# A hybrid decoder trunk: the even layer's mixer over all tokens at once, heads between later column blocks, three classical tiles instead of six

## The chip, the cores and the metric

The kernel runs on one core of one Trainium2 chip. The metric is the device time of one execution in microseconds. Three runs of the kernel before are given, and one execution was recorded by the hardware profiler.

## What is computed

The input x has 1024 tokens of 1024 channels, all in float32. Two layers follow each other, then a last RMS norm. Layer 0 has a mixer with one input projection of 2560 columns: differential attention (four heads, each with two softmax maps over 64 channels, and values of 128 channels) and four groups of spatial gating (a 128x128 lower-triangular product over each chunk of 128 tokens). Layer 1 has a convolution mixer. After each mixer comes a gated feed-forward block. The parts that the change touches, cut from the reference:

```python
def even_mixer(h, ...):
    proj = h @ w_in
    q, k, v = ...                       # 512, 512 and 512 columns
    uz = jax.nn.gelu(proj[..., o2:])    # 1024 columns
    u, z = jnp.split(uz, 2, axis=-1)
    q, k = apply_rope(q, cos, sin), apply_rope(k, cos, sin)
    o = diff_attention(q, k, v, lam)    # softmax(q1 k1) - lam * softmax(q2 k2), causal, times v
    o = rms_norm(o, subln_g) * (1.0 - lambda_init)
    g = spatial_gating(u, z, sg_ln_g, sg_ln_b, sg_w, sg_b)
    return jnp.concatenate([o, g], axis=-1) @ w_out

def conv_ffn(h, w_up, dw_w, dw_b, w_down):
    hh = causal_dwconv(h @ w_up, dw_w, dw_b)
    a, gate = jnp.split(hh, 2, axis=-1)
    return (a * jax.nn.silu(gate)) @ w_down

for l in range(2):
    x = x + mixer(rms_norm(x, norm_mix_g[l]), ...)
    x = x + conv_ffn(rms_norm(x, norm_ffn_g[l]), ...)
return rms_norm(x, final_norm_g)
```

## The kernel before

Tokens stand in eight tiles of 128 (`t`), four to a chunk `c` of 512. Every float32 matmul is made of three: each operand is split into a rounded high part (a cast on ACT, L144) and the rest (a subtraction on POOL or DVE, L148), and the products high-high, high-low and low-high are added in PSUM (`PASSES`).

*Column blocks.* `col_steps` streams a block of 512 weight columns: four loads of 1024 values a partition (`raw`), split into eight tiles `hl`, of which there are eight (`WHL`). Then each token tile is one step: 24 matmuls of 128x512 into one `bank` (L269), and a function `fin` that takes the bank away. A `fin` may return a second part (transposes and stores for queries and keys, L378 and L382; the gating product, L508). It is held in the list `delayed` and is done after three more steps, or when `flush` empties the list. The second parts write to one buffer `sec` and from there to DRAM. Each block of the mixer (values, two of queries and keys, two of gates) is streamed once for chunk 0 and once for chunk 1.

*Heads.* `att_steps(c, h)` has four units, one for each token tile of the chunk. A unit makes the scores of both maps on PE (L432, L435, mask L434), takes the maximum on DVE (L438, L440), the exp on ACT (L446), combines the maps on DVE (L455), transposes on PE (L462), copies on ACT (L463), and multiplies with the values on PE (L466). The first unit of a head calls `flush` and loads queries, keys and values from DRAM.

*Order of the work.* `interleave(main, shadow, start, end)` calls the steps of `main` and, spread over the given share of them, those of `shadow`. A scheduler then sets the order in which each engine's instructions stand. In layer 0: values for chunk 0, queries and keys, gates, the norm of chunk 1; then the heads of chunk 0 beside four blocks; then the output projection of chunk 0, the norm of its rows, the gates of chunk 1 and the first four feed-forward tiles, beside the heads of chunk 1.

*Feed-forward.* `head_steps` makes a tile of 128 hidden channels in the classical way: gate and value, 24 matmuls each for each chunk (L306), so 96. `pair_steps` makes a tile with seven products of 12 matmuls (L677), so 84. It needs sums and differences of normed rows; `combos` loads the rows `xd`, scales them again with the kept factors `rn`, and forms them. The first `PRE0` tiles of layer 0 are classical.

```python
    interleave(qk_steps(0, 1) + v_steps(1) + qk_steps(1, 0) + qk_steps(1, 1),
               [f for h in range(4) for f in att_steps(0, h)] + og_steps(0), 0.0, 0.85)
    open_psum(2)
    interleave(out_steps(ab_w_out[0], ogT, 0, x_from(x_in)) +
               norm_steps(0, xtile, norm_ffn_g[0], hF0, hb=sbank, keep=rn[0], spill=xd[0]) +
               gate_steps(1, 0) + gate_steps(1, 1) + head_steps(0, 0, hF0, order(0)[:PRE0 - PRE0_LATE]),
               [f for h in range(4) for f in att_steps(1, h)] + [flush] + og_steps(1), 0.0, 0.9)
```

`open_psum(wide)` divides the eight banks of PSUM anew: with 1 there are four single banks for column steps, one double and two small ones; with 2 there are two single banks and two double ones (the scores stand in a double one).

Of the kernel before, what the change touches and what calls it, by code (L numbers as in the profile page):

```python
# [10 lines left out]
F32 = mybir.dt.float32  # L11
# [9 lines left out]
P = 128  # L21
# [25 lines left out]
PRE0, PRE0_LATE = 6, 2  # L47
# [12 lines left out]
def trunk_kernel(ctx: ExitStack, tc: tile.TileContext, x, norm_mix_g, norm_ffn_g, ab_w_in, ab_w_out,  # L60
# [68 lines left out]
    def rows_to_cols(dst, loads):  # L129

        n = sum(c for _, c in loads)
        st = wk.tile([P, P], F32, tag="rtc", name="rtc", bufs=2)
        r = 0
        for ap, c in loads:
            nc.sync.dma_start(out=st[r:r + c, :], in_=ap)
            r += c
        ps = sbank()
        nc.tensor.transpose(ps[:, :n], st[:n, :], ident[:n, :n])
        nc.vector.tensor_copy(out=dst, in_=ps[:, :n])
# [51 lines left out]
    def rms_tile(xt, gain, junk, out=None, keep=None):  # L191
        ss = small.tile([P, 1], F32, tag="ss", name="ss")
        nc.scalar.activation(out=junk, in_=xt.rearrange("p (j c) -> p j c", c=P), func=AF.Square, accum_out=ss)
        r = rstd_of(ss, 1.0 / D, 1, "n", keep)
# [32 lines left out]
    def norm_steps(c, src, gain_ap, dst, in_place=False, hb=None, keep=None, spill=None):  # L227


        def f(t):  # L230
# [5 lines left out]
            if spill is not None:  # L236
                nc.sync.dma_start(out=spill[t * P:(t + 1) * P, :], in_=xt)
            xn = rms_tile(xt, dst["gain"], junk, xt if in_place else None, None if keep is None else keep[:, t:t + 1])
# [9 lines left out]
    def col_steps(load, hT, c, fin, early=False):  # L248
# [15 lines left out]
        def mm(t, late):  # L264
            ps = bank()
            n = 0
            for d in range(DT):
                for sa, sw in PASSES:
                    nc.tensor.matmul(ps, lhsT=hT[c][:, sa, d, tok(t)], rhs=units[d][:, sw, :],  # L269
# [6 lines left out]
        steps = [lambda t=t: f(t) for t in range(c * TPC, (c + 1) * TPC)]  # L276
# [46 lines left out]
    rn = [const.tile([P, NT], F32, name=f"rn{l}") for l in range(2)]  # L323
# [18 lines left out]
    def v_steps(c, early=False):  # L342
        return col_steps(plain_cols(w_in, 1024), hT0, c, v_fin, early)

    ns, vs = norm_steps(0, x_load, norm_mix_g[0], hT0, True, sbank), v_steps(0, True)
    ns[0]()
    vs[0]()
    for i in range(1, TPC):
        ns[i]()
        vs[i]()  # L350
    vs[TPC]()
# [128 lines left out]
    def gate_fin(j):  # L480
        st = {}

        def f(ps, t):
            if t % TPC == 0:
# [34 lines left out]
    def qk_steps(c, hp):  # L519
        return col_steps(two_cols(w_in, hp * 256, 512 + hp * 256), hT0, c, qk_fin(hp))  # L520

    def gate_steps(c, j):
        return col_steps(two_cols(w_in, 1536 + j * 256, 2048 + j * 256), hT0, c, gate_fin(j))
# [12 lines left out]
    def out_steps(w, actT, c, prepare, after=None):  # L536
# [9 lines left out]
        return [f for half in range(2) for f in col_steps(plain_cols(w, half * 512), actT, c, fin(half))]  # L546
# [66 lines left out]
    def combos(l, hT, up_pool):  # L613
# [4 lines left out]
        def f(k):  # L618
            if k == 0:
                T["gain"] = load_gain(norm_ffn_g[l])  # L620
# [258 lines left out]
    mf = wk.tile([P, P], F32, tag="rtc", name="rtc", bufs=2)  # L879
# [26 lines left out]
    for g in range(4):  # L906
        st = wk.tile([P, P], F32, tag="rtc", name="rtc", bufs=2)
# [163 lines left out]
    for c in range(NCH):  # L1071
# [12 lines left out]
    interleave(norm_steps(0, xtile, norm_ffn_g[1], hF1, keep=rn[1], spill=xd[1]) +  # L1084
# [4 lines left out]
               norm_steps(1, xtile, norm_ffn_g[1], hF1, keep=rn[1], spill=xd[1]), 0.0, 0.3)  # L1089
# [81 lines left out]
```

## Time and profile before

| | us |
|---|---|
| median of three runs (2303.5 to 2309.1) | 2305.05 |
| the profiled execution's own time | 2305.63 |
| its span | 2303.9 |
| PE busy | 2147.5 (93%) |
| DVE busy | 1601.8 (70%) |
| ACT busy | 1120.9 (49%) |
| POOL busy | 1002.2 (43%) |

A matmul's busy time counts its whole passage, and matmuls follow each other faster than that, so a stretch in which PE is always busy can still hold slow matmuls: the granted clock of the stretch tells. Times inside the execution are counted from the span's start.

### The profile page before, as it was taken

The page shows a single profiled execution, that of the slowest core. Times are in us where ns is not written, and L with a number is a line of the kernel's source. Part 1 is how long each engine was busy: PE and PEld are TensorE (multiplying, and loading weights), DVE is VectorE, ACT ScalarE, POOL GpSimd, SP SyncE. Part 2 cuts the span into 40 slices and gives each one's busy share as a digit, 9 for nine tenths or more (in the row PEclk, how much of TensorE's full clock was granted, in tenths as well). Part 3 has the DMA queues.
Part 4 walks back from the last instruction along what each step waited for, and adds up shares of the span by engine and source line. Part 5 has one row for each costly group of instructions (what it writes and reads, how often), then busy time and mean ns, then how long its engine had stood idle before and what let it go on. Part 6 is the DMA issues. An engine that isn't in the chain of part 4 may idle for free.

```text
span 2303.9 us, 28559 instructions
## 1 busy us (share of the span) xinstructions
PE 2147.5 (93%) x9882; PEld 1760.4 (76%) x9882; DVE 1601.8 (70%) x2787; ACT 1120.9 (49%) x1971; POOL 1002.2 (43%) x824
## 2 busy tenths in 40 slices
PE   8889879989999999999999969979989899999987
PEld 6677768778788888888887758858768788878876
DVE  6675747864875555555699968996576576766676
ACT  4344535642445444443556566555533444544354
POOL 3312311222635444445579836974555455530011
PEclk9999979999999999999999979979989999999999
DMA  7736545435432222275634422523535233339423
GB/s 240 217 101 202 172 151 185 156 97 193 142 100 80 92 84 82 85 247 191 192 113 125 152 78 83 155 69 115 183 118 161 78 111 96 116 118 328 128 89 112
DMA packets 299953, 318.80 MB, mean 138 GB/s; under 512 B 12445, under 2 KB 221601, under 8 KB 299297
## 3 DMA queue, kind: packets, MB, share of 16 engines
q1 hardware_dynamic: 293920, 302.30, 41.0%
q0 software_dynamic: 5888, 14.68, 2.1%
q8 instruction: 78, 1.28, 0.2%
q14 instruction: 67, 0.54, 0.1%
HBM read 253.76 MB, written 63.18 MB: 138 GB/s over the span
## 4 chain that ended last, share of the span: by engine, by line
PE 70%; DVE 18%; issue 4%; DMA 3%; ACT 3%; POOL 3%; SPq 0%; ACTq 0%; DVEq 0%; POOLq 0%
PE bank L677 25%; PE bank L306 14%; PE bank L269 11%; PE bank L821 7%; PE bank L858 6%; DVE sbank L1006 5%; DVE hl L148 2%; PE sbank L821 2%; DVE y L182 1%; POOL ap L1003 1%; PE sbank L466 1%; POOL hl L148 1%; DVE xn L197 1%; PE sbank L213 1%; ACT hl L144 1%
## 5 line engine op out<-in xcount | busy, mean ns | idle before, releaser
L148 POOL TENSOR_TENSOR hl<-raw,hl 128x512 fp32r<-128x512 f32 x456 | 632.0, 1404 | 506.4 <-ACT hl L144 479.5
L306 PE MATMUL bank<-big,hl 128*128 128x512 f32 x2112 | 498.8, 395 | 9.5 <-DVE big L225 3.4
L144 ACT CAST hl<-raw 128x512 fp32r<-128x512 f32 x616 | 358.2, 618 | 233.9 <-PE bank L858 68.9
L306 PEld LDWEIGHTS bank<-big,hl 128*128 128x128 f32 x2112 | 396.9, 190 | 95.6 <-DVE big L225 5.0
L269 PE MATMUL bank<-hl,big 128*128 128x512 f32 x1728 | 427.4, 402 | 20.5 <-POOL hl L148 9.2
L269 PEld LDWEIGHTS bank<-hl,big 128*128 128x128 f32 x1728 | 325.9, 192 | 91.2 <-POOL hl L148 9.8
L677 PE MATMUL bank<-big,hl 128*128 128x512 f32 x1440 | 342.9, 390 | 0.1
L677 PEld LDWEIGHTS bank<-big,hl 128*128 128x128 f32 x1440 | 270.0, 188 | 58.2 <-ACT hl L144 0.5
L677 PE MATMUL bank<-t,hl 128*128 128x512 f32 x1080 | 264.2, 394 | 6.0 <-ACT hl L144 6.0
L1006 DVE SCALAR_TENSOR_TENSOR sbank<-yb,cw,sbank 128x512 f32<-128x512 f32 x352 | 248.1, 748 | 6.0 <-ACT sbank L995 3.2
L685 DVE SCALAR_TENSOR_TENSOR bank<-row,dw,bank 128x1024 f32<-128x1024 f32 x120 | 154.5, 1287 | 140.6 <-ACT bank L683 138.1
L858 PE MATMUL bank<-hl 128*128 128x512 f32 x1056 | 247.1, 392 | 2.5 <-DVE hl L148 2.2
L677 PEld LDWEIGHTS bank<-t,hl 128*128 128x128 f32 x1080 | 203.6, 189 | 51.2 <-ACT hl L144 6.3
L148 DVE TENSOR_TENSOR hl<-raw,hl 128x512 fp32r<-128x512 f32 x160 | 169.6, 1080 | 93.1 <-ACT hl L144 92.8
L858 PEld LDWEIGHTS bank<-hl 128*128 128x128 f32 x1056 | 196.4, 188 | 48.8 <-DVE hl L148 8.4
L821 PE MATMUL bank<-hl 128*128 128x512 f32 x726 | 176.8, 398 | 10.4 <-DVE s L731 4.4
L821 PEld LDWEIGHTS bank<-hl 128*128 128x128 f32 x726 | 139.4, 193 | 42.3 <-issue 5.8
L1003 POOL TENSOR_TENSOR ap<-ap,pr 128x512 f32<-128x512 f32 x112 | 153.8, 1373 | 34.5 <-ACT ap L998 20.7
L144 ACT CAST hl<-s 128x512 fp32r<-128x512 f32 x101 | 62.8, 621 | 137.6 <-DVE s L700 75.3
L579 DVE SCALAR_TENSOR_TENSOR s<-bank,dw,s 128x510 f32<-128x510 f32 x112 | 83.5, 745 | 52.9 <-ACT s L576 51.4
L1002 ACT ACTIVATE pr<-yb,cw 128x512 f32<-128x512 f32 x112 | 80.8, 723 | 70.2 <-POOL ap L1003 70.0
L1112 POOL TENSOR_TENSOR xr<-xr,gain 128x512 f32<-128x512 f32 x10 | 14.5, 1479 | 202.3 <-ACT xn L1104 176.8
(206 smaller groups left out, 2565.8 us busy)
## 6 DMA issues: line engine op xcount, KB each, us to landing
raw<-in_ffn_w_up SPq DMA_DIRECT2D x116, 512.0 KB, 4.1
raw<-in_ffn_w_down SPq DMA_DIRECT2D x44, 512.0 KB, 3.8
raw<-phd SPq DMA_DIRECT2D x44, 512.0 KB, 4.8
ph<-phs SPq DMA_DIRECT2D x33, 512.0 KB, 3.5
raw<-in_ab_w_in SPq DMA_DIRECT2D x64, 256.0 KB, 3.5
raw<-in_conv_w_in SPq DMA_DIRECT2D x32, 512.0 KB, 4.1
qd<-s SPq DMA_DIRECT2D x32, 256.0 KB, 2.9
qk<-qd POOLq DMA_DIRECT2D x8, 1024.0 KB, 7.0
```

Of the source, the lines that this page charges most:

```text
L144: nc.scalar.copy(out=hl_hi, in_=raw)
L148: eng.tensor_sub(out=hl_lo, in0=raw, in1=hl_hi.bitcast(F32))
L269: nc.tensor.matmul(ps, lhsT=hT[c][:, sa, d, tok(t)], rhs=units[d][:, sw, :], start=(n == 0), stop=(n == 3 * DT - 1))
L306: nc.tensor.matmul(ps, lhsT=hv[d // 4][:, sw, d % 4, :], rhs=hT[:, sa, d, :], start=(n == 0), stop=(n == 3 * DT - 1))
L579: nc.vector.scalar_tensor_tensor(out=y[:, sh:], in0=ps[:, :CH - sh], scalar=dw[:, k, ct:ct + 1], in1=y[:, sh:], op0=ALU.mult, op1=ALU.add)
L677: nc.tensor.matmul(ps, lhsT=hv[:, sw, d, :], rhs=B[n](sa, d), start=(start and i == 0), stop=(i == 11), skip_group_check=True)
L685: nc.vector.scalar_tensor_tensor(out=y, in0=r[:, k:k + S], scalar=dw[:, k, ct:ct + 1], in1=y, op0=ALU.mult, op1=ALU.add)
L821: nc.tensor.matmul(ps[k], lhsT=a[:, sa, k * P:(k + 1) * P], rhs=w[:, sw, :], start=(n in (5, 2, 1) and js[0] == 0 and i == 0), stop=(end a ...
L858: nc.tensor.matmul(ps, lhsT=phs[i][:, sa, k * P:(k + 1) * P], rhs=wds[i][:, sw, :], start=(dp == 0 and n == 0), stop=(dp == DP - 1 and n = ...
L1002: nc.scalar.activation(out=pr, in_=ys[ct][:, k:k + CH], func=AF.Copy, scale=cw[:, ct, k:k + 1])
L1003: nc.gpsimd.tensor_add(out=st["ap"], in0=st["ap"], in1=pr)
L1006: nc.vector.scalar_tensor_tensor(out=st["acc"], in0=ys[ct][:, k:k + CH], scalar=cw[:, ct, k:k + 1], in1=st["acc"], op0=ALU.mult, op1=ALU.add)
```

## The change

The mixer's blocks are streamed once, each for all eight token tiles: values beside the norm of all eight, then queries and keys of the first two heads, and from then on the heads of both chunks, head by head, beside the second block of queries and keys and the two blocks of gates. PSUM is divided anew before the heads. The output projections and the norms follow after the heads. Three tiles of layer 0's feed-forward are classical instead of six. The norm writes its result to a DRAM tensor `xnd`, and `combos` loads that instead of scaling again; its four subtractions are all on DVE, where two were on POOL. There are four `rtc` buffers instead of two.

```diff
-PRE0, PRE0_LATE = 6, 2
+PRE0 = 3
...
-        st = wk.tile([P, P], F32, tag="rtc", name="rtc", bufs=2)
+        st = wk.tile([P, P], F32, tag="rtc", name="rtc", bufs=4)
...
             if spill is not None:
-                nc.sync.dma_start(out=spill[t * P:(t + 1) * P, :], in_=xt)
-            xn = rms_tile(xt, dst["gain"], junk, xt if in_place else None, None if keep is None else keep[:, t:t + 1])
+                nc.sync.dma_start(out=spill[0][t * P:(t + 1) * P, :], in_=xt)
+            xn = rms_tile(xt, dst["gain"], junk, xt if in_place else None)
+            if spill is not None:
+                nc.sync.dma_start(out=spill[1][t * P:(t + 1) * P, :], in_=xn)
             transpose_split(xn, dst[c], t, hb)
...
-    def col_steps(load, hT, c, fin, early=False):
+    def col_steps(load, hT, ts, fin, early=False):
...
-                    nc.tensor.matmul(ps, lhsT=hT[c][:, sa, d, tok(t)], rhs=units[d][:, sw, :],
+                    nc.tensor.matmul(ps, lhsT=hT[t // TPC][:, sa, d, tok(t)], rhs=units[d][:, sw, :],
...
-        steps = [lambda t=t: f(t) for t in range(c * TPC, (c + 1) * TPC)]
+        steps = [lambda t=t: f(t) for t in ts]
...
-    ns, vs = norm_steps(0, x_load, norm_mix_g[0], hT0, True, sbank), v_steps(0, True)
+    ns = [f for c in range(NCH) for f in norm_steps(c, x_load, norm_mix_g[0], hT0, True, sbank)]
+    vs = col_steps(plain_cols(w_in, 1024), hT0, range(NT), v_fin, True)
...
-                nc.sync.dma_start(out=xt, in_=xd[l][t * P:(t + 1) * P, :])
-                nc.vector.scalar_tensor_tensor(out=xt, in0=xt, scalar=rn[l][:, t:t + 1], in1=T["gain"],
-                                               op0=ALU.mult, op1=ALU.mult)
+                nc.sync.dma_start(out=xt, in_=xnd[t * P:(t + 1) * P, :])
...
-            nc.gpsimd.tensor_sub(out=xb[:, :512], in0=xb[:, 512:], in1=xb[:, :512])
+            nc.vector.tensor_sub(out=xb[:, :512], in0=xb[:, 512:], in1=xb[:, :512])
...
-            nc.gpsimd.tensor_sub(out=xa[:, 512:], in0=xa[:, 512:], in1=xb[:, 512:])
+            nc.vector.tensor_sub(out=xa[:, 512:], in0=xa[:, 512:], in1=xb[:, 512:])
...
-    run(qk_steps(0, 0))
-    run(gate_steps(0, 0))
-    interleave([f for pair in zip(gate_steps(0, 1), norm_steps(1, x_load, norm_mix_g[0], hT0, True, sbank)) for f in pair],
-               const_steps())
-    interleave(qk_steps(0, 1) + v_steps(1) + qk_steps(1, 0) + qk_steps(1, 1),
-               [f for h in range(4) for f in att_steps(0, h)] + og_steps(0), 0.0, 0.85)
+    interleave(qk_steps(0), const_steps())
     hF0 = {}
-    flush()
     open_psum(2)
-    interleave(out_steps(ab_w_out[0], ogT, 0, x_from(x_in)) +
-               norm_steps(0, xtile, norm_ffn_g[0], hF0, hb=sbank, keep=rn[0], spill=xd[0]) +
-               gate_steps(1, 0) + gate_steps(1, 1) + head_steps(0, 0, hF0, order(0)[:PRE0 - PRE0_LATE]),
-               [f for h in range(4) for f in att_steps(1, h)] + [flush] + og_steps(1), 0.0, 0.9)
-    run(out_steps(ab_w_out[0], ogT, 1, x_from(x_in)))
-    interleave(head_steps(0, 0, hF0, order(0)[PRE0 - PRE0_LATE:PRE0]),
-               norm_steps(1, xtile, norm_ffn_g[0], hF0, keep=rn[0], spill=xd[0]), 0.0, 0.3)
+    att = [att_steps(c, h) for h in range(4) for c in range(NCH)]
+    g1 = gate_steps(1)
+    interleave(qk_steps(1) + gate_steps(0) + g1[:TPC], [f for a in att[:7] for f in a], 0.08, 1.0)
+    interleave(g1[TPC:] + [flush], att[7] + og_steps(0), 0.0, 1.0)
+    interleave(out_steps(ab_w_out[0], ogT, 0, x_from(x_in)), og_steps(1), 0.0, 0.8)
+    interleave(out_steps(ab_w_out[0], ogT, 1, x_from(x_in)),
+               norm_steps(0, xtile, norm_ffn_g[0], hF0, hb=sbank, spill=(xd[0], xnd)), 0.0, 0.8)
     M.close()
     open_psum(1)
+    interleave(head_steps(0, 0, hF0, order(0)[:PRE0]),
+               norm_steps(1, xtile, norm_ffn_g[0], hF0, spill=(xd[0], xnd)), 0.0, 0.4)
```

How instructions stand after the scheduler, at two places. On PE, inside a head of the second chunk, before the change (L269 are column matmuls of the output projection, L432 and L435 scores, L462 transposes, L466 products with the values):

```order
L269 MATMUL bank<-hl,big 128x512 x6
L466 MATMUL sbank<-vh,aT 128x128 x4
L462 MATMUL sbank<-ident,e 128x128 x4
L269 MATMUL bank<-hl,big 128x512 x13
L432 MATMUL bank_3721<-qk 128x448
L435 MATMUL bank_3721<-qk 128x448
L432 MATMUL bank_3721<-qk 128x448
L434 LDWEIGHTS identb
```

After the change, on PE, the same part of such a head (the second head's last unit):

```order
L462 MATMUL sbank<-ident,e 128x128 x4
L466 MATMUL sbank<-vh,aT 128x128
L432 MATMUL bank_2763<-qk 128x512
L435 MATMUL bank_2763<-qk 128x512
L432 MATMUL bank_2763<-qk 128x512
L434 LDWEIGHTS identb
L434 MATMUL bank_2763<-maskb,identb 128x128
L435 MATMUL bank_2763<-qk 128x512
L462 MATMUL sbank<-ident,e 128x128 x2
L432 MATMUL bank_2772<-qk 128x512
```

Column matmuls stood between a head's transposes and its next scores, and now they don't. They stand in bursts at other places, as here, in the third head (L271 is L269 before, L508 the gating product):

```order
L508 MATMUL bank<-held,sgwT 128x128 x2
L271 MATMUL bank<-hl,big 128x512 x47
L462 MATMUL sbank<-ident,e 128x128 x3
L271 MATMUL bank<-hl,big 128x512
L508 MATMUL bank<-held,sgwT 128x128 x2
L466 MATMUL sbank<-vh,aT 128x128 x3
L462 MATMUL sbank<-ident,e 128x128 x4
```

So a whole head of the second chunk may pass with hardly a column matmul, and then two steps of a block follow at once. On ACT, in the fourth head of the first chunk after the change (L492 is the gates' gelu, L446 the heads' exp; each ACT_TABLE_LOAD changes the function table):

```order
L492 ACT_TABLE_LOAD
L492 ACTIVATE held<-bank 128x512
L463 COPY aT<-sbank 128x512
L463 COPY aT<-sbank 128x384
L446 ACT_TABLE_LOAD
L446 ACTIVATE e,sm<-bank_3677,nm 128x256 x2
L492 ACT_TABLE_LOAD
L492 ACTIVATE held<-bank 128x512
```

Gates and heads alternate on ACT: up to the first pair tile there are 27 table loads, where there were 16.

## Rows read from the trace of the kernel before

**Rows 1.** The page: span, and shares of the chain of waits by engine.

```profile
span 2303.9 us, 28559 instructions
...
PE 70%; DVE 18%; issue 4%; DMA 3%; ACT 3%; POOL 3%; SPq 0%; ACTq 0%; DVEq 0%; POOLq 0%
```

**Rows 2.** Busy time by stretch (us); columns are named in its first line.

```profile
core 0: us, PE busy (x) PEld busy (x) DVE busy (x) ACT busy (x) POOL busy (x), PEclk, DMA share, GB/s
0.00:136.60 136.60, 117.38 (x556) 95.43 (x557) 93.84 (x299) 57.83 (x106) 42.45 (x45) 0.98 0.66 209
136.60:516.00 379.40, 333.90 (x1814) 278.67 (x1813) 248.35 (x613) 188.37 (x426) 89.97 (x80) 0.93 0.50 155
136.60:328.00 191.40, 157.67 (x831) 129.96 (x830) 108.08 (x238) 79.35 (x214) 46.30 (x46) 0.88 0.56 173
328.00:486.00 158.00, 146.23 (x824) 123.04 (x823) 127.68 (x352) 92.48 (x180) 34.66 (x27) 0.98 0.46 145
375.00:475.00 100.00, 88.23 (x498) 74.00 (x496) 89.57 (x282) 66.95 (x124) 25.11 (x20) 0.97 0.52 161
516.00:682.70 166.70, 161.93 (x768) 133.35 (x768) 113.25 (x181) 65.70 (x107) 69.82 (x50) 1.00 0.47 149
750.00:1050.00 300.00, 300.00 (x1316) 246.78 (x1315) 171.75 (x200) 143.38 (x220) 126.02 (x118) 1.00 0.36 121
```

**Rows 3.** Waits of PE, 136.6 to 516 us: us in total, times, longest.

```profile
PE sbank L466 <- DVE big L217: 7.8, 1, 7.8
...
PE bank L378 <- ACT s L379: 7.3, 2, 6.1
...
PE bank L432 <- ACT e L446: 6.7, 5, 2.9
...
PE bank L382 <- DVE s L364: 5.1, 1, 5.1
```

**Rows 4.** Timeline of PE: start, us, instructions, idle before and its releaser.

```profile
11.03 8.25 PE L269 MATMUL bank<-hl,big 128*128 128x512 f32 x24 [0.62 <-ACT big L216]
...
110.77 1.65 PE L269 MATMUL bank<-hl,big 128*128 128x512 f32 x3 [5.51 <-POOL hl L148]
...
136.60 0.31 PE L432 MATMUL bank<-qk 128*128 128x128 f32 x1
...
515.74 15.24 PE L306 MATMUL bank<-big,hl 128*128 128x512 f32 x66
...
530.82 1.91 PE L221 MATMUL bank<-ident,ot 128*128 128x128 f32 x16
...
682.71 1.64 PE L677 MATMUL bank<-big,hl 128*128 128x512 f32 x6
```

**Rows 5.** Timeline of DVE: the heads' first maximum and the last two.

```profile
141.21 0.42 DVE L440 TENSOR_REDUCE nm<-bank 128x2 f32<-128x256 f32 x1
...
484.93 2.35 DVE L438 TENSOR_REDUCE nm<-bank 128x1 f32<-128x1024 f32 x2
```

**Rows 6.** Groups of DVE and POOL to 690 us: busy us, mean ns, idle before.

```profile
L438 DVE TENSOR_REDUCE nm<-bank 128x1 f32<-128x1024 f32 x8 | 9.7, 1218 | 2.8 <-PE bank L435 2.8
...
L384 DVE COPY sec<-bank 128x512 f32<-128x512 f32 x16 | 11.0, 686 | 15.4 <-DMA kd<-sec 9.3 <-PE bank L382 6.1
...
L629 DVE SCALAR_TENSOR_TENSOR s<-s,rn,gain 128x1024 f32<-128x1024 f32 x4 | 7.2, 1798 | 0.2 <-DMA s<-xd 0.2
...
L629 DVE SCALAR_TENSOR_TENSOR xa<-xa,rn,gain 128x1024 f32<-128x1024 f32 x4 | 6.1, 1536 | 0.3 <-DMA gain<-in_norm_ffn_g 0.3
...
L635 DVE TENSOR_TENSOR s<-s,xa 128x512 f32<-128x512 f32 x4 | 4.9, 1221 | 0.3 <-POOL s L634 0.3
...
L636 POOL TENSOR_TENSOR xa<-xa,s 128x512 f32<-128x512 f32 x4 | 6.1, 1530 | 0.6 <-DVE s L635 0.6
```

**Rows 7.** Timeline of ACT at a table load.

```profile
391.23 1.28 ACT L492 ACT_TABLE_LOAD   x1
392.53 0.60 ACT L492 ACTIVATE held<-bank 128x512 f32<-128x512 f32 x1
```

More of the change, by code (lines that the diff above doesn't have):

```diff
@@ L189, in rstd_of, with rms_tile @@
         return out
-    def rms_tile(xt, gain, junk, out=None, keep=None):
+    def rms_tile(xt, gain, junk, out=None):
         ss = small.tile([P, 1], F32, tag="ss", name="ss")
         nc.scalar.activation(out=junk, in_=xt.rearrange("p (j c) -> p j c", c=P), func=AF.Square, accum_out=ss)
-        r = rstd_of(ss, 1.0 / D, 1, "n", keep)
+        r = rstd_of(ss, 1.0 / D, 1, "n")
         if out is None:
@@ L225, in transpose_split, with norm_steps @@
         nc.vector.tensor_sub(out=dst[:, 1, :, tok(t)], in0=psv, in1=hi.bitcast(F32))
-    def norm_steps(c, src, gain_ap, dst, in_place=False, hb=None, keep=None, spill=None):
+    def norm_steps(c, src, gain_ap, dst, in_place=False, hb=None, spill=None):
         def f(t):
@@ L322, in trunk_kernel @@
     phs = dram.tile([P, 7, HH, CH], F32, name="phs")
-    rn = [const.tile([P, NT], F32, name=f"rn{l}") for l in range(2)]
+    xnd = dram.tile([S, D], F32, name="xnd")
     M = ExitStack()
@@ L340, in v_fin @@
         nc.sync.dma_start(out=vd[t * P:(t + 1) * P, :], in_=vt)
-    def v_steps(c, early=False):
-        return col_steps(plain_cols(w_in, 1024), hT0, c, v_fin, early)
-    ns, vs = norm_steps(0, x_load, norm_mix_g[0], hT0, True, sbank), v_steps(0, True)
+    ns = [f for c in range(NCH) for f in norm_steps(c, x_load, norm_mix_g[0], hT0, True, sbank)]
+    vs = col_steps(plain_cols(w_in, 1024), hT0, range(NT), v_fin, True)
     ns[0]()
     vs[0]()
-    for i in range(1, TPC):
+    for i in range(1, NT):
         ns[i]()
         vs[i]()
-    vs[TPC]()
+    vs[NT]()
     def qk_fin(hp):
@@ L483, in f @@
         def f(ps, t):
-            if t % TPC == 0:
+            if t == 0:
                 lngb = mp.tile([P, 2, 256], F32, tag="lngb", name="lngb", bufs=1)
@@ L517, in gate_fin, with qk_steps, gate_steps @@
         return f
[L519 to L523, printed above, removed]
+    def qk_steps(hp):
+        return col_steps(two_cols(w_in, hp * 256, 512 + hp * 256), hT0, range(NT), qk_fin(hp))
+    def gate_steps(j):
+        return col_steps(two_cols(w_in, 1536 + j * 256, 2048 + j * 256), hT0, range(NT), gate_fin(j))
     ogT = {}
@@ L545, in fin @@
             return f
-        return [f for half in range(2) for f in col_steps(plain_cols(w, half * 512), actT, c, fin(half))]
+        return [f for half in range(2) for f in col_steps(plain_cols(w, half * 512), actT, range(c * TPC, (c + 1) * TPC), fin(half))]
     dws, halos = [], []
@@ L619, in f @@
             if k == 0:
-                T["gain"] = load_gain(norm_ffn_g[l])
                 T["row"] = []
@@ L878, in trunk_kernel @@
     nc.vector.tensor_copy(out=identb, in_=ident)
-    mf = wk.tile([P, P], F32, tag="rtc", name="rtc", bufs=2)
+    mf = wk.tile([P, P], F32, tag="rtc", name="rtc", bufs=4)
     nc.gpsimd.memset(mf, 0.0)
@@ L906, in trunk_kernel @@
     for g in range(4):
-        st = wk.tile([P, P], F32, tag="rtc", name="rtc", bufs=2)
+        st = wk.tile([P, P], F32, tag="rtc", name="rtc", bufs=4)
         nc.sync.dma_start(out=st, in_=sg_w[0, g])
@@ L926, in taps @@
         def taps(c):
-            st = wk.tile([CW, P], F32, tag="rtc", name="rtc", bufs=2)
+            st = wk.tile([CW, P], F32, tag="rtc", name="rtc", bufs=4)
             nc.sync.dma_start(out=st, in_=conv_dw_w[0, :, c * P:(c + 1) * P])
@@ L1083, in trunk_kernel @@
     interleave(out_steps(conv_w_out[0], acT, 0, lambda c: None, out_bias(0)) + ci[4:], dws1[:len(dws1) // 2], 0.0, 1.0)
-    interleave(norm_steps(0, xtile, norm_ffn_g[1], hF1, keep=rn[1], spill=xd[1]) +
+    interleave(norm_steps(0, xtile, norm_ffn_g[1], hF1, spill=(xd[1], xnd)) +
                head_steps(1, 0, hF1, order(1)[:PRE1 - PRE1_LATE]),
@@ L1088, in trunk_kernel @@
     interleave(head_steps(1, 0, hF1, order(1)[PRE1 - PRE1_LATE:PRE1]),
-               norm_steps(1, xtile, norm_ffn_g[1], hF1, keep=rn[1], spill=xd[1]), 0.0, 0.3)
+               norm_steps(1, xtile, norm_ffn_g[1], hF1, spill=(xd[1], xnd)), 0.0, 0.3)
     C.close()
```

## Prediction

> **What bounds the kernel now.** I read the page's first part and its chain: the tensor engine (PE) is busy 93% of the span and holds 70% of the chain, DVE 18% [rows 1]. So time is won where PE waits or repeats work. Next I read the busy time by stretch [rows 2]. From 750 us on PE has no idle time at all; that stretch the change leaves alone. What it rebuilds ends when the first pair tile starts, at 682.7 us [rows 4]. I cut this part in three: S1 up to the first score matmul of a head at 136.6, S2 up to the last product of a head with its values at 516.0, S3 up to 682.7 [rows 2, 4]. In S2 PE is busy 334 of 379 us at a mean granted clock of 0.93, in its first half 0.88. The waits view shows what stopped it: chains through DVE and ACT, a few us each [rows 3].
>
> To compare S2 before and after I need PE's bare work. A 128x512 matmul takes 0.229 us: 66 of them fill the 15.08 us from 515.74 to 530.82, and 1316 fill 300 us [rows 2, 4]. Counting every PE instruction of S2 in the old order (0.229 us per 512 columns, 0.08 to 0.16 us for a transpose or small product) gives 289 us. The 379 us are then 289 of work, 45.5 idle, and some 45 of busy time beyond the work: the half clock. The same count on DVE, at the median duration of each kind, gives 253 us; the trace shows 248 [rows 2]. So the counts can be trusted to 2%.
>
> **The change part by part.**
> *Fewer weight blocks.* Five blocks of the mixer are loaded and split once instead of twice: 20 loads of 512 KB, 40 casts on ACT and 40 subtractions on POOL and DVE go. The matmuls stay. This work lies beside PE; PE saw it only at a block's start, as in the 5.5 us for POOL's `hl` [rows 4].
>
> *S1.* The order up to the first score holds the same 408 column matmuls as before, 108 us of PE work against 107. Before, S1 took 136.6: 8.5 us of start, some 4.5 around the first 24 matmuls, which took 8.25 us instead of 5.5 [rows 4], and 16 at block starts and at half clock. Now two block starts are left, not four. I take 8.5 + 4.5 + 108 + 5 = 126; ends 121 (no loss) and 137 (the same losses).
>
> *S2, the main term.* All 32 head units now stand between 23 column steps, 552 column matmuls; before they had 864 beside them. PE's work in S2 falls from 289 to 213 us, DVE's only from 253 to 234: heads 116, gates 82, rotary 25, the rest 11 [prices as in rows 6]. **DVE becomes the larger load**, and ACT has 161. They also come in turns: bursts of 47 to 72 matmuls, then units with hardly any. So I took the time between two successive maximum reductions (47 stretches) as the larger of what PE and DVE do in it by the order. The sum is 231 us. The same sum over the old order is 296, and there the trace shows 345 us, from 141.2 to 486.1, the start of the last of two [rows 5]: a ratio of 1.17. By halves: up to 328 it is 187 measured against 142 (1.31), after that 158 against 154 (1.03). I take 1.17, since the new order has both kinds of place: 231 x 1.17 = 269. To this come 4.6 us from first score to first reduction as before, and 26 from the last reduction to the last product (25 of PE work; before 29.9 measured for 28.7). S2 = 300, S1 + S2 = 426 against 516. Ends: 268 with 1.03, 334 with 1.31.
>
> *A function switch on ACT.* The gates' gelu now alternates with the heads' exp: 27 table loads up to the pair tiles instead of 16. In the trace a load takes 1.28 us and the gelu starts 1.30 after it [rows 7], so 11 more are 14 us of ACT, inside the 161 and beside DVE's 234; I take nothing. The Trainium skill (ScalarE: Activation LUTs, What ACT_TABLE_LOAD costs) adds a drain and gives 2.66 us for each switch. The row shows no such drain, so here the measurement decides; by the page's figure 25 loads in S2 would put about 34 us more on ACT, an estimate from that page.
>
> *S3.* PE's work rises from 162 to 171 us: out_steps for both halves now lie here whole, 192 column matmuls more, against three classical tiles less. Before, S3 took 166.7, 5 above its work, at full clock [rows 2]. I take 171 + 5 = 176. The order puts head matmuls between the four normed tiles, so that cover stays; DVE has 109 us here.
>
> *Three tiles.* As classical tiles they cost 3 x 96 matmuls, as pair tiles 3 x 84: 36 x 0.229 = 8 us less. As the 57.5 us of pair tiles (3 x 84 x 0.228) they stand behind S3.
>
> *Normed rows in DRAM.* Per layer eight 512 KB writes are added, and the loads of combos come from there. On SP each reload stands right behind its write, so the up-projection loads behind it wait some us; they are issued at least two column steps (11 us) ahead, and the DMA engines are 47% busy in S3 [rows 2]. I take 0; ends 0 and +4. In combos eight DVE scalings go (13.3 us) and eight half-row subtractions move from POOL (1.5 us each) to DVE, where such a one takes 0.7 to 1.2 [rows 6]: DVE has 4 to 8 us less. PE hardly waited there, so 0 to -2 in each layer; I take 0. More `rtc` buffers end waits of a few us in S2: inside the ratio.
>
> **Sum.** 126 + 300 + 176 + 57.5 = 659.5 against 682.7: 23 us less. From the profiled execution's 2305.6 that is 2282.4; it lies 0.6 above the median shown, so I say **2282**.
>
> **Rivals.** *DVE runs full.* Where DVE was densest, 375 to 475 us, it was busy 89.6% [rows 2]. With 234 us of work S2 would be 261, by the ratio 1.03 268: some 32 less than I take, 2250. For it: the new order gives DVE something in nearly every stretch. Against: a head's chain reduction, exp, combine, transpose, product has to turn around between engines.
>
> *The gain is eaten by the flush.* Each head load empties the list of held second parts, and these share one `sec` buffer, whose write must land first. Before, five in a row made PE wait 5.1 and 6.1 us, and DVE's copies 9.3 us for that buffer [rows 3, 6]. Now there are eight flushes. If each costs 3 us more than the ratio holds, S2 is 325 and the time 2306: no change. Against: 15 of the 26 second parts in S2 are small gate tiles, spread in the order.
>
> *Too little cover (the other side).* Between two bursts stands a whole head of the second chunk, for which PE has some 15 us of work in small pieces, each waiting for exp or for DVE; then its clock falls, and the next burst of 47 matmuls (11 us) starts at half clock, while DVE starves. The first half of S2 shows such a place: clock 0.88, ratio 1.31. With it throughout, S2 is 334 and the time 2316: slower. It decides from a ratio of 1.27, S2 = 323. For it: 312 column matmuls, 71 us of cover, have left S2. Against: the second half of S2, with DVE at 81%, held a clock of 0.98.
>
> *The switch costs more than the load.* If each switch held up ACT for as long again as its load (1.3 us), and ACT set the pace at each of the 25 in S2, that would be 33 us more and the time 2315. The row at 391 us speaks against it [rows 7]. (The page of the Trainium skill named above would lead one to this case.)
>
> **How the numbers follow.** My forecast 0.47 (its own range 2264 to 2298), DVE full 0.17, eaten 0.13, too little cover 0.20, the switch 0.03. About 0.3% (7 us) is what a measurement of this kernel can tell from no change. The forecast and the first rival are faster: 0.64; eaten is the same: 0.13; the last two are slower: 0.23. The range reaches from 2246 (DVE full, with S1 at its lower end) to 2318 (1.31, with 2 us from combos or SP), leaving out what goes beyond on either side.
>
> **What would show it.** First score near 126 us, last product of a head near 426, first pair tile near 602; then all later stretches as before, shifted, with 57 us more pair tiles. In S2 DVE busy 75 to 80%, PE 70 to 80%, the granted clock 0.85 to 0.95; 27 table loads of 1.28 us. A clock under 0.85 in S2 with PE waiting for ACT's exp or DVE's combine shows too little cover; waits of DVE for `sec` shows the flush. Wrong altogether would be a first pair tile later than 625 us, or a difference that arises behind it.

## The result, and the profile after

The changed kernel takes **2281.5 us** (median of four runs, 2278.2 to 2284.7), the kernel before 2306.0 beside it: a ratio of 0.9893 [0.9872, 0.9914]. The forecast was 2282. Its profiled execution took 2278.2 us, its span is 2275.8, 28.1 us less than before. By the prediction's stretches (us, from the traces):

| | before | forecast | after |
|---|---|---|---|
| S1, to the first score | 136.6 | 126 | 128.7 |
| S2, to the last product with values | 379.4 | 300 | 281.9 |
| S3, to the first pair tile | 166.7 | 176 | 185.9 |
| layer 0's pair tiles | 314.1 | 371.6 | 372.0 |
| all that follows | 1307.1 | 1307.1 | 1307.3 |

The total was right; S2 came out 18 us shorter than I said and S3 10 us longer. Busy time by stretch of the changed kernel, with the columns of [rows 2]:

```profile
core 0: us, PE busy (x) PEld busy (x) DVE busy (x) ACT busy (x) POOL busy (x), PEclk, DMA share, GB/s
0.00:128.68 128.68, 114.45 (x558) 92.16 (x559) 66.48 (x167) 50.44 (x98) 31.37 (x42) 1.00 0.56 180
128.68:410.60 281.92, 257.08 (x1454) 212.41 (x1455) 197.74 (x636) 156.86 (x354) 38.78 (x43) 0.95 0.49 153
128.68:270.00 141.32, 127.50 (x705) 103.96 (x706) 88.05 (x227) 70.43 (x177) 24.98 (x31) 0.92 0.58 175
270.00:410.60 140.60, 129.58 (x751) 108.44 (x750) 109.69 (x409) 86.42 (x178) 13.80 (x12) 0.99 0.40 130
410.60:596.50 185.90, 174.36 (x829) 144.28 (x827) 118.04 (x221) 70.26 (x115) 54.17 (x37) 0.98 0.50 166
```

In S2 PE is busy 257 of 282 us, 91%, and DVE 198, 70%. I had forecast the reverse: DVE the larger load with 234, busy 75 to 80%, and PE 70 to 80%. The boundaries, on the timeline of PE (as [rows 4]):

```profile
10.89 7.14 PE L271 MATMUL bank<-hl,big 128*128 128x512 f32 x24 [0.42 <-ACT big L216]
...
128.68 0.30 PE L432 MATMUL bank<-qk 128*128 128x128 f32 x1 [2.66 <-DMA qk<-qd]
...
409.55 1.06 PE L466 MATMUL sbank<-vh,aT 128*128 128x128 f32 x8
...
596.51 2.43 PE L674 MATMUL bank<-big,hl 128*128 128x512 f32 x10
```

What PE waited for in S2 (us in total, times, longest; as [rows 3]):

```profile
PE bank L432 <- ACT e L446: 11.2, 13, 1.7
PE bank L271 <- DVE sec L384: 3.6, 1, 3.6
PE sbank L466 <- ACT aT L463: 3.0, 4, 1.3
PE bank L432 <- DMA qk<-qd: 2.7, 1, 2.7
```

and in S3:

```profile
PE bank L221 <- DVE big L225: 5.6, 2, 2.9
PE bank L508 <- DVE held L504: 4.7, 1, 4.7
```

The single waits of 5 to 8 us in [rows 3] are gone. The largest items left in S2 are thirteen short waits for exp and one for the buffer `sec`. In S3 three waits, two at the norm's transposes (L221) and one at a gating product (L508), hold 10.3 of the 11.5 us in which PE is idle.

### The profile page after: what moved, and what is told of

The parts are those of the page before. It is cut to its first block, busy times and chain, and to the rows that moved or that the text cites. A ratio compares the mean times of both kernels' runs of the same rounds, so it can differ in the third digit from the quotient of the medians.

```text
span 2275.8 us, 28260 instructions
## 1 busy us (share of the span) xinstructions
PE 2136.1 (94%) x9846; PEld 1749.4 (77%) x9846; DVE 1561.3 (69%) x2758; ACT 1114.6 (49%) x1942; POOL 937.1 (41%) x788
## 3 DMA queue, kind: packets, MB, share of 16 engines
q8 instruction: 78, 1.28, 0.2%
## 5 line engine op out<-in xcount | busy, mean ns | idle before, releaser
L148 POOL TENSOR_TENSOR hl<-raw,hl 128x512 fp32r<-128x512 f32 x424 | 583.3, 1395 | 481.1 <-ACT hl L144 460.6
L271 PE MATMUL bank<-hl,big 128*128 128x512 f32 x1728 | 423.1, 400 | 10.7 <-DVE sec L384 3.6
L308 PE MATMUL bank<-big,hl 128*128 128x512 f32 x1824 | 426.6, 393 | 5.1 <-DVE yb L974 2.1
L144 ACT CAST hl<-raw 128x512 fp32r<-128x512 f32 x564 | 326.2, 617 | 199.2 <-PE bank L855 69.3
L308 PEld LDWEIGHTS bank<-big,hl 128*128 128x128 f32 x1824 | 342.2, 189 | 79.1 <-DVE yb L974 3.8
L271 PEld LDWEIGHTS bank<-hl,big 128*128 128x128 f32 x1728 | 325.1, 192 | 82.3 <-ACT big L144 4.2
L674 PE MATMUL bank<-big,hl 128*128 128x512 f32 x1584 | 376.7, 390 | 0.0
L674 PEld LDWEIGHTS bank<-big,hl 128*128 128x128 f32 x1584 | 297.2, 188 | 63.2 <-POOL hl L148 0.4
L674 PE MATMUL bank<-t,hl 128*128 128x512 f32 x1188 | 291.3, 394 | 6.0 <-ACT hl L144 6.0
L682 DVE SCALAR_TENSOR_TENSOR bank<-row,dw,bank 128x1024 f32<-128x1024 f32 x132 | 169.8, 1287 | 160.2 <-ACT bank L680 157.6
L674 PEld LDWEIGHTS bank<-t,hl 128*128 128x128 f32 x1188 | 224.6, 189 | 55.9 <-ACT hl L144 6.3
L148 DVE TENSOR_TENSOR hl<-raw,hl 128x512 fp32r<-128x512 f32 x140 | 154.6, 1127 | 95.9 <-ACT hl L144 95.8
L818 PEld LDWEIGHTS bank<-hl 128*128 128x128 f32 x726 | 139.1, 192 | 42.2 <-ACT hl L144 5.0
L996 POOL TENSOR_TENSOR ap<-ap,pr 128x512 f32<-128x512 f32 x112 | 155.4, 1388 | 38.4 <-ACT ap L991 24.8
L144 ACT CAST hl<-s 128x512 fp32r<-128x512 f32 x110 | 68.4, 621 | 154.8 <-DVE s L697 89.4
L699 POOL TENSOR_TENSOR s<-raw,s 128x512 f32<-128x512 f32 x33 | 42.9, 1301 | 131.1 <-DVE hl L148 131.1
```

The source lines that it names most:

```text
L144: nc.scalar.copy(out=hl_hi, in_=raw)
L148: eng.tensor_sub(out=hl_lo, in0=raw, in1=hl_hi.bitcast(F32))
L271: nc.tensor.matmul(ps, lhsT=hT[t // TPC][:, sa, d, tok(t)], rhs=units[d][:, sw, :], start=(n == 0), stop=(n == 3 * DT - 1))
L308: nc.tensor.matmul(ps, lhsT=hv[d // 4][:, sw, d % 4, :], rhs=hT[:, sa, d, :], start=(n == 0), stop=(n == 3 * DT - 1))
L674: nc.tensor.matmul(ps, lhsT=hv[:, sw, d, :], rhs=B[n](sa, d), start=(start and i == 0), stop=(i == 11), skip_group_check=True)
L682: nc.vector.scalar_tensor_tensor(out=y, in0=r[:, k:k + S], scalar=dw[:, k, ct:ct + 1], in1=y, op0=ALU.mult, op1=ALU.add)
```

## Why DVE's load was misjudged

My count of DVE's work added the median durations of its instructions. This is DVE's timeline at the heads' first maximum, near their end, and at the last maximum (start, us, instruction; as [rows 5]):

```profile
129.56 0.42 DVE L440 TENSOR_REDUCE nm<-bank 128x2 f32<-128x256 f32 x1 [4.86 <-PE bank L435]
...
375.81 0.21 DVE L182 SCALAR_TENSOR_TENSOR y<-q,v,y 128x1 f32<-128x1 f32 x1
375.94 0.21 DVE L453 SCALAR_TENSOR_TENSOR cf<-sm,nlam,rs 128x1 f32<-128x1 f32 x1
376.07 1.08 DVE L438 TENSOR_REDUCE nm<-bank 128x1 f32<-128x896 f32 x1
377.07 0.15 DVE L188 RECIPROCAL y<-y 128x2 f32<-128x2 f32 x1
377.15 1.00 DVE L455 SCALAR_TENSOR_TENSOR e<-e,cf 128x768 f32<-128x768 f32 x1
...
381.95 1.22 DVE L438 TENSOR_REDUCE nm<-bank 128x1 f32<-128x1024 f32 x1
```

From 375.81 on each instruction starts before the one ahead of it has ended: the two of 0.21 us stand 0.13 apart, the reciprocal of 0.15 starts 1.00 after the reduction of 1.08 and holds up the next one by 0.08. The sum of the durations is more than the time that they fill. Adding count times mean over all groups of DVE in S2 gives 234.7 us, where the engine is busy 197.7. My count of 234 hit the sum, and the sum is not the load. Before, I had tested the count against the busy time of S2, 253 against 248, and trusted it to 2%. That was chance: the durations there add up to 281, so the count was 28 short, and the overlap was 33. Two errors of nearly one size cancelled. The Trainium skill gives a reason (Perfetto Trace Analysis, Optimizing Scalar/DVE Operations): for the fixed overhead of an instruction the profiled time is about twice the engine-busy time, "since the write-acknowledgement half overlaps with the next instruction". The rows here agree in kind, with 0.21 us shown and 0.13 between starts; that the overlap is the write's acknowledgement no run here shows.

## The experiments

Each kernel ran beside the kernel before on the same chip; the ratio to it has its 95% interval. Times are medians, and "more" and "less" are against the changed kernel's 2281.5 where nothing else is said. The kernel before had medians of 2305.4 to 2307.7 in the different groups of runs, so a difference of 2 or 3 us between groups says nothing.

**1. More cover in S3: six classical tiles.**

```diff
-PRE0 = 3
+PRE0 = 6
```

> The changed kernel with six classical tiles in layer 0 again. My theory: a classical tile costs 12 matmuls of 0.229 us more than a pair tile and nothing else, so 3 x 12 x 0.229 = 8 us more, 2290. Rival: the three tiles were cover for the norm of chunk 1 and for combos, where the changed kernel loses some 15 us beside PE's work instead of 5; then they give back up to 10 us and the time is 2279 to 2283.

Measured: 2287.1 us, 0.9918 [0.9906, 0.9930]. In the trace S3 grows by 66.8 us and the pair tiles shrink by 57.9, so three tiles are worth 8.9 us; the medians say 6, and the intervals of the two kernels overlap a little. The added 288 matmuls are 66 us of work, so S3 was not short of cover, and the term of 8 us stands.

**2. Every block streamed twice, in the new order.**

```diff
+    halves = lambda cols, fin, early=False: (col_steps(cols, hT0, range(TPC), fin, early) +
+                                            col_steps(cols, hT0, range(TPC, NT), fin))
...
-        return col_steps(two_cols(w_in, hp * 256, 512 + hp * 256), hT0, range(NT), qk_fin(hp))
+        return halves(two_cols(w_in, hp * 256, 512 + hp * 256), qk_fin(hp))
```

(and so for values and gates)

> The changed kernel with each of the mixer's five blocks streamed and split twice, once for tiles 0 to 3 and once for 4 to 7; the order of the steps stays. My theory: loads and splits lie beside PE and the gain came from where the heads stand, so 0 to 6 us more, 2281 to 2288. Rival: the halved stream is the gain, since PE waited at block starts; then most of the 25 us come back, 2298 to 2306.

Measured: 2292.5 us, 0.9947 [0.9933, 0.9961]: 11 more. In S2 (line numbers are two higher here):

```profile
128.50:424.70 296.20, 262.63 (x1452) 214.73 (x1452) 213.06 (x645) 171.02 (x378) 57.66 (x55) 0.95 0.53 165
```

```profile
PE bank L434 <- ACT e L448: 15.6, 14, 2.2
```

PE's instructions are the same, yet S2 is 14.3 us longer: PE is busy 5.6 more and idle 8.7 more, while DVE and ACT have some 15 us more each. The work that I priced at nothing, as lying beside PE, is worth 11 us, between the two numbers expected. PE's wait for ACT's exp rose from 11.2 to 15.6 us, half of the added idle time; that the added casts on ACT, standing in front of the exp, are the reason is likely but not shown.

**3. The old combos, without normed rows in DRAM.**

```diff
-                nc.sync.dma_start(out=xt, in_=xnd[t * P:(t + 1) * P, :])
+                nc.sync.dma_start(out=xt, in_=xd[l][t * P:(t + 1) * P, :])
+                nc.vector.scalar_tensor_tensor(out=xt, in0=xt, scalar=rn[l][:, t:t + 1], in1=T["gain"],
...
-            nc.vector.tensor_sub(out=xb[:, :512], in0=xb[:, 512:], in1=xb[:, :512])
+            nc.gpsimd.tensor_sub(out=xb[:, :512], in0=xb[:, 512:], in1=xb[:, :512])
```

> The changed kernel with combos as before: rows loaded from xd and scaled again on DVE, two of the four subtractions on POOL, no normed rows in DRAM. My theory: PE hardly waits there, so no change within 3 us, 2279 to 2285. Rival: DVE is what holds combos up in the shorter stage, so the old form costs 4 to 10 us, 2286 to 2292.

Measured: 2282.8 us, 0.9910 [0.9895, 0.9924]. No difference that these runs can tell: this part of the change is worth nothing, as priced.

**4. The kernel before with three classical tiles** (the heads' share of that interleave moved with them):

```diff
-PRE0, PRE0_LATE = 6, 2
+PRE0, PRE0_LATE = 3, 1
...
-               [f for h in range(4) for f in att_steps(1, h)] + [flush] + og_steps(1), 0.0, 0.9)
+               [f for h in range(4) for f in att_steps(1, h)] + [flush] + og_steps(1), 0.0, 1.09)
```

> The kernel before with three classical tiles instead of six and all else as before (two of them beside the heads of chunk 1, one beside the norm). By the count of matmuls alone: 8 us less than before, 2298. Rival: the tiles were cover for the heads of chunk 1 (the stretch then holds 24 main steps instead of 28), the gain is eaten, 2303 to 2312.

Measured: 2326.0 us, 1.0088 [1.0075, 1.0101]: 20 us slower than the kernel before, further than either expected. S3, and PE's waits in it:

```profile
515.20:647.30 132.10, 106.56 (x489) 87.89 (x490) 77.89 (x129) 40.31 (x64) 40.76 (x29) 0.87 0.42 134
```

```profile
PE bank L221 <- DMA ot<-og: 9.4, 1, 9.4
PE bank L306 <- DVE big L225: 8.1, 1, 8.1
PE bank L221 <- DVE xn L197: 6.7, 3, 3.3
```

66 us of tiles left PE's queue (3 x 96 x 0.229): 263 of the 288 matmuls stood in S3, 25 in S2. But S2 fell by 0.6 us and S3 by 34.6; PE is idle for 25.5 us of S3, where it was 4.8, and the granted clock falls from 1.00 to 0.87. In the old order these tiles were the cover of the wait for the gated rows and of the norm. In the new one S3 holds both halves of the output projection, and does without. So in the old order, placed like this, the 8 us of experiment 1 were not to be had; other places for the heads beside fewer tiles were not tried.

**5. More work for PE: eight matmuls ahead of each of the 24 later steps,** whose results are overwritten.

```diff
+            for d in range(extra):
+                nc.tensor.matmul(ps, lhsT=hT[t // TPC][:, 0, d, tok(t)], rhs=units[d][:, 0, :], start=True, stop=True)
```

> The changed kernel with 8 matmuls of 128x512 more in each of the 24 column steps beside the heads (results overwritten by the step itself): 192 x 0.229 = 44 us of PE work. If DVE sets the pace of that stretch, as I predicted: at most 15 us more, 2282 to 2297. If PE itself does (it is busy 257 of 282 us there): 35 to 44 us more, 2316 to 2326.

Measured: 2320.8 us, 1.0049 [1.0032, 1.0066]: 39 more.

```profile
127.70:445.20 317.50, 293.27 (x1602) 242.66 (x1602) 197.02 (x623) 144.19 (x339) 36.20 (x40) 0.96 0.42 131
445.20:640.30 195.10, 181.46 (x866) 151.16 (x865) 125.01 (x233) 74.89 (x121) 59.13 (x41) 0.97 0.50 167
```

S2 alone grows by 35.6 us, but it doesn't hold the same instructions: eight of the added matmuls stand in S1, and 11 column matmuls and some 26 small products have moved from S2 to S3. Over all three stretches the count is fair: the first pair tile starts at 640.3 us against 596.5, which is 43.8 later for 44.0 us of added work (192 x 0.229). Were DVE the pace, the work would first have filled PE's idle time, 24.8 us in S2 before; 24.2 are still there. **PE sets the pace in S2**, with short waits for the heads' chain on top; the theory behind my forecast of it falls here.

**6. Less work for DVE: the gates' scale and shift on POOL.**

```diff
-            nc.vector.tensor_mul(out=zn, in0=zn, in1=lngb[:, 0, :])
-            nc.vector.tensor_add(out=zn, in0=zn, in1=lngb[:, 1, :])
+            nc.gpsimd.tensor_mul(out=zn, in0=zn, in1=lngb[:, 0, :])
+            nc.gpsimd.tensor_add(out=zn, in0=zn, in1=lngb[:, 1, :])
```

> The changed kernel with the gates' last scale and shift on POOL, which is nearly idle there: 32 operations of 0.42 us, 13 us of DVE less. If DVE sets the pace of the heads' stretch: 8 to 13 us less, 2268 to 2274. If PE does, or the chain from engine to engine: within 3 us, 2278 to 2285.

Measured: 2279.7 us, 0.9875 [0.9857, 0.9893]. S2:

```profile
128.60:408.70 280.10, 258.19 (x1452) 212.47 (x1452) 191.37 (x602) 151.75 (x350) 62.68 (x73) 0.95 0.49 152
```

That is within the scatter of the changed kernel; S2 is 280.1 against 281.9. The counterpart of experiment 5: taking from DVE gives next to nothing. It takes less from DVE than I said, too: the 30 operations that S2 holds add up to 12.5 us, but DVE's busy time falls by 6.4.

**7. No function switch: identity in place of gelu.**

```diff
-            nc.scalar.activation(out=uz, in_=ps, func=AF.Gelu_apprx_tanh)
+            nc.scalar.activation(out=uz, in_=ps, func=AF.Identity)
```

> The changed kernel with the identity in place of gelu, so that exp keeps its table: 25 table loads less, 32 us of ACT. It leaves out the gelu. My theory: ACT has room, so 0 to 5 us less, 2276 to 2282. Rival: switches hold up the heads' chain, 15 to 35 us less, 2246 to 2266.

Measured: 2270.4 us, 0.9836 [0.9821, 0.9851]: 11 less. The groups of table loads up to the pair tiles, in the changed kernel (count, busy us, mean ns, idle before):

```profile
L492 ACT ACT_TABLE_LOAD x13 | 16.7, 1283 | 3.8 <-PE bank L271 3.6
L446 ACT ACT_TABLE_LOAD x12 | 15.4, 1283 | 5.2 <-DVE e L455 2.3 <-DVE y L175 1.7 <-DVE q L179 1.1
L193 ACT ACT_TABLE_LOAD x1 | 1.3, 1283 | 0.8 <-PEq L1150 0.8
L592 ACT ACT_TABLE_LOAD x1 | 1.3, 1283 | 4.3 <-DVE halo L585 4.3
```

The 27 loads of the forecast are there, and the first two groups are gone in this run. ACT's busy time in S2 falls from 156.9 to 124.2 us:

```profile
130.70:403.10 272.40, 255.15 (x1454) 211.52 (x1455) 198.28 (x637) 124.20 (x329) 39.06 (x43) 0.96 0.51 157
```

```profile
PE bank L432 <- ACT e L446: 4.7, 7, 1.1
```

That is 32.7 us for 25 loads, 1.31 each, the load's own 1.28 and no second part as long. S2 falls by 9.5 us and PE's wait for exp from 11.2 to 4.7. So a third of the loads' time is on the path and the rest beside PE. My nothing was wrong by some 10 us. By the Trainium skill's 2.66 us for a switch (ScalarE: Activation LUTs, What ACT_TABLE_LOAD costs) ACT would have lost some 66 us here, an estimate from that page; the measurement says half of that.

**8. Two buffers under `sec`** (room for it from two `rtc` in place of four):

```diff
-                kst = mp.tile([P, 4, P], F32, tag="sec", name="sec", bufs=1)
+                kst = mp.tile([P, 4, P], F32, tag="sec", name="sec", bufs=2)
...
-        st = wk.tile([P, P], F32, tag="rtc", name="rtc", bufs=4)
+        st = wk.tile([P, P], F32, tag="rtc", name="rtc", bufs=2)
```

> The changed kernel with two sec buffers for the second parts, at the price of two rtc buffers instead of four. DVE waited 12 us in total for that buffer, 10.5 of them at the first flush, where PE waited 3.6. If that flush holds up the stretch: 4 to 10 us less, 2271 to 2277. If not: within 3 us, 2278 to 2285; the fewer rtc buffers may cost 1 to 3 us before the heads.

Measured: 2271.1 us, 0.9841 [0.9827, 0.9856]: 10 less than the changed kernel. Its first flush, on DVE's timeline of the changed kernel:

```profile
151.64 0.69 DVE L384 COPY sec<-bank 128x512 f32<-128x512 f32 x1
...
156.51 0.69 DVE L384 COPY sec<-bank 128x512 f32<-128x512 f32 x1 [1.30 <-DMA kd<-sec]
...
167.70 0.69 DVE L384 COPY sec<-bank 128x512 f32<-128x512 f32 x1 [10.50 <-DMA kd<-sec]
```

and of this one:

```profile
154.56 0.69 DVE L384 COPY sec<-bank 128x512 f32<-128x512 f32 x1
157.14 0.69 DVE L384 COPY sec<-bank 128x512 f32<-128x512 f32 x1 [0.59 <-PE bank L382]
159.94 0.69 DVE L384 COPY sec<-bank 128x512 f32<-128x512 f32 x1 [0.65 <-PE bank L382]
```

Three copies stand 16 us apart in the one, 5.4 in the other: DVE waited 10.5 us for the buffer's write to DRAM, with PE's next step behind it (3.6 us of PE's waits above). The buffer makes every copy wait for the store before it, but this store was slow besides: issued at 157.23 us, it held the copy until 167.70, where the stores from this buffer in experiment 9's trace land after 1.7 to 9.2 us, the median after 3.1. Why this one was slow stays open.

**9. Its control: two `rtc` alone.**

> The changed kernel with two buffers under `rtc` in place of four, `sec` left alone: the control for the run with two `sec`, which had both edits. Theory (the gain of 10 to 12 us came from `sec`; fewer `rtc` buffers cost a little ahead of the first score, 131.3 against 128.7 there): 2281 to 2287, first score at 130 to 133. Rival (the gain came from the changed addresses or start of the program, and not from `sec`): 2270 to 2274.

Measured: 2275.7 us, 0.9866 [0.9852, 0.9881], between the two expected; the first score is at 128.1, not 130 to 133. Up to the first pair tile no stretch of its trace differs by more than about 2 us from the changed kernel (S1 128.1, S2 279.8, and DVE's longest wait for `sec` is 9.4 us), so I can't name a place for the 6 us; the runs of the two kernels overlap (2272.5 to 2281.0, 2278.2 to 2284.7). Of the 5 us between the two profiled executions 2 lie ahead of the first pair tile and 3 behind layer 0's pair tiles, where neither `sec` nor `rtc` is used, and where the profiled executions of all these kernels spread from 1303 to 1308 us. So part of the 6 us is scatter. What is left for `sec` is 5 us by the medians, 4 by S2:

```profile
131.30:407.30 276.00, 255.02 (x1453) 211.34 (x1454) 198.28 (x637) 157.69 (x354) 38.60 (x43) 0.97 0.51 157
128.10:408.00 279.90, 252.91 (x1455) 209.53 (x1456) 197.73 (x637) 156.80 (x354) 39.22 (x43) 0.98 0.51 157
```

(experiment 8, then this one). The 10 of experiment 8 are not all its own. But S2 is 272.9 to 275.9 us in the three kernels with two `sec` (experiments 8, 11 and 12), and 279.8 to 284.1 in the five with one and otherwise nearly the same S2 (the changed kernel and experiments 1, 3, 6 and 9). Pairs that differ in `sec` alone or in `sec` and `rtc` give 4 us (experiments 9 and 8) and 6 us (6 and 11): that is what the buffer is worth in S2.

**10. The kernel before with two `sec`** (one `rn` for both layers makes the room).

> The kernel before with two buffers under `sec`, paid for by one `rn` column table for both layers: does the one buffer hold up the old order too (rows 6 show it as the largest ending of VectorE's idle time before the second halves' copies, 9.3 us)? Theory: it does as much there, 6 to 12 us, so 2294 to 2300, and the change's own gain over a kernel with two buffers is the same 20 to 25 us. Rival (in the old order the flush is covered, or the time goes into the next wait): 2302 to 2308, and the buffer is a wait that the longer runs of steps brought in.

Measured: 2296.9 us, 0.9962 [0.9948, 0.9975]: 11 less than the kernel before, beside it 2307.6. S2 falls from 379.4 to 371.6, while DVE's waits for the buffer fall only from 9.3 to one of 6.0 us. So the buffer seems to have held up the old order too, by about as much; no run has the edit to `rn` alone, and experiment 9 shows that such a side edit can go with 6 us, so the share of `sec` is not shown here. With two `sec` on both sides the new order is 26 us faster (2271.1 against 2296.9), where theory had 20 to 25.

**11. Experiments 6 and 8 together.**

> The changed kernel with two buffers under `sec` (and two instead of four under `rtc`) as in the run with two `sec`, and the gates' scale and shift on GpSimd as in the run with the gates there: the two runs that gained 10 to 12 us and about 4 us. Theory (TensorE sets the pace, and the `sec` buffer held it up by itself): the first gain stays and the second, within noise alone, adds 0 to 4: 2266 to 2272, a ratio of 0.982 to 0.985. Rival (both gains were the same wait of VectorE, got rid of twice): no better than either alone, 2271 to 2276. Rival 2 (GpSimd, with one buffer more to run ahead into, delays the second half's copies): 2278 to 2285.

Measured: 2269.1 us, 0.9835 [0.9822, 0.9847], as the theory has it. It is 2 us under experiment 8, whose interval it overlaps, so that POOL's share adds anything is not shown. Against experiment 6, which differs only in `sec` and `rtc`, it is 11 less, and the intervals stand apart.

**12. And the second norm's transposes through two small banks.**

```diff
-               norm_steps(1, xtile, norm_ffn_g[0], hF0, spill=(xd[0], xnd)), 0.0, 0.4)
+               norm_steps(1, xtile, norm_ffn_g[0], hF0, hb=sbank, spill=(xd[0], xnd)), 0.0, 0.4)
```

> The run with two `sec` and the gates' scale and shift on GpSimd, and besides, the second chunk's feed-forward norm turns its rows through two single small banks instead of one double bank. In S3 of the changed kernel the tensor engine waited twice, 2.9 and 2.7 us, for VectorE's reading of that double bank. Theory (these waits lie on the path, since the tensor engine is the bound in S3 too): S3 falls by 4 to 6 us, 2263 to 2266. Rival (the next tile's norm, square root and scaling on ACT and VectorE are what is late, whatever the bank): within 2 us of the run without this edit, 2267 to 2271.

Measured: 2266.9 us, 0.9826 [0.9811, 0.9840]. In the trace S3 falls from 188.2 (experiment 11) to 183.7:

```profile
404.50:588.24 183.74, 174.98 (x821) 145.14 (x820) 114.17 (x219) 69.49 (x116) 55.58 (x39) 0.97 0.49 164
```

```profile
PE bank L508 <- POOL held L504: 5.2, 1, 5.2
PE sbank L213 <- DVE big L217: 2.7, 1, 2.7
```

Of the two waits the second is gone. The first is still there, 2.7 us at the same place (536 us), now for DVE's reading of a small bank (L217): there DVE is late with either kind of bank, and why is not shown. PE's idle time in S3 falls by 3.3 us, from 12.0 to 8.8, and not by the 5.7 of both waits. By the medians, 2.3 us apart, the two kernels can't be told apart. This is the fastest version measured, 14.6 us under the changed kernel; the intervals of their ratios stand apart.

## Why the prediction was right, point by point

*S1: right.* 128.7 for 126; PE waits 2.7 us for the first head's load of queries and keys, which the forecast did not have.

*S2: the right direction by a wrong reason.* The failed step is "DVE becomes the larger load" (198 us busy, not 234, and PE 257), and with it the sum of the larger of PE and DVE, stretch by stretch, times 1.17. From the first maximum at 129.56 us to the start of the last at 381.95 the trace has 252.4 us, 1.09 times my 231. The sum was too high where DVE's overstated durations were the larger, and the ratio, taken from an order with other errors and with waits of 5 to 8 us that are gone, didn't carry over; which of the two weighs more no run shows. What holds instead: PE busy 257 us and 25 us of short waits, most for ACT. Its 213 us of bare work again became 44 more of busy time, as before (45). The 552 column matmuls account for 12.7 of it: their group is busy 139.1 us, 0.252 each and not 0.229. The prediction calls those 45 us the half clock, and that can't be: a mean clock of 0.95 over 282 us, where the levels are full and half, takes at most 14 us of work away, and 0.93 over 379 us at most 27 (estimates from the granted clock in the rows of S2). So some 30 of the 44, and 18 or more of the 45, are something else, such as small products that I priced too low; how they divide stays open.

*The clock: right.* It was 0.95 in S2, at the upper end of what I named; 0.92 and 0.99 by halves, 0.88 and 0.98 before [rows 2].

*S3: too low by 10.* PE's work was right, 174 for 171. Its idle time is 11.5 us where I took 5 over from before. At 416.2 us the last gating product waits 4.7 for its scale and shift on DVE, just after the heads; and the norm's transposes wait twice for the one double bank. I had noted that head matmuls stand between the normed tiles and called the cover the same. By experiment 12 the double bank is the cause of one of these two waits; the other is there with small banks too. The words of the sum don't give its number either: S3 lost 167 matmuls of classical tiles and not 288, since 121 of them stood in S2 before; with 192 column matmuls and some 35 small products more that does make the 9 us I added.

*Tiles, normed rows: right.* The pair tiles grew by 57.9 us for 57.5, and the normed rows gave nothing.

*The switch: a term of nothing that was 10 us.* The load takes 1.28 us as said, and ACT is busy only 157 of 282 us; but PE's scores wait for exp, so a load in front of an exp can be on the path. S2's forecast was high enough to hide it.

*Weight blocks: nothing, and 11 us* (experiment 2), probably for the same reason.

*Where the gain comes from.* Taken out of the changed kernel one by one, streaming once is worth 11 us (experiment 2), the three tiles 6 to 9 (experiment 1), the normed rows nothing (experiment 3), and four `rtc` buffers nothing or less (experiment 9). Of the 24.5 us that leaves 5 to 8 for the new place of the heads. This is a subtraction: no run moves the heads alone, and experiment 4 shows that such parts don't simply add up.

*The rivals.* DVE full: its time was not reached, and DVE was busy 70%. Flush: the place is real, one wait of 10.5 us on DVE, but worth some 4 to 6 and not 25. Too little cover: the whole heads with hardly a column matmul are there, yet the clock held; it decided from a ratio of 1.27, and the ratio was 1.09. Something like it happened to S3 of the old order when its cover was taken away (experiment 4). The switch at twice its load: no second part of that length is seen, and ACT doesn't set the pace throughout, with 11 us for all 25 loads (experiment 7).

So errors of opposite sign made the total good, to 4 us in the profiled execution: S2 18 us too high, S1 and S3 together 13 too low. That the total hit is luck. The sum of parts was less certain than its result looks.

## What to carry to other kernels

Take an engine's load from its busy time and the distance between starts, not from the sum of its instructions' durations, and test a count on each kind of instruction, not only on a total that two errors can leave unharmed. Work called free because it lies beside the bound engine has to be checked against the chain that the bound engine waits for: here a third of the table loads' time was on it. A stretch that ends with a given instruction can hold other work in another kernel; count its instructions before dividing, or take a stretch that holds all of the change. Where a list of held parts is emptied at once, one buffer in front of a DMA serialises them; look for a store that the next copy waits for.

## What was unexpected on the chip

Small DVE instructions shown with 0.21 us follow each other in 0.13. One store out of a 256 KB buffer took some 10 us to free it, where the median of such stores was 3.1. And taking three tiles of 66 us out of the old order gave back only 35.2 in S2 and S3 together, with 20.8 us more of PE's idle time in S3 and the granted clock there at 0.87.
